# GpSimd's DMA queue in written order: two quarters' sums fetched inside the last period, two behind it

## The chip, the cores and the metric

The kernel runs on one core of one Trainium2 chip. Its time is the device time of one execution in microseconds (us); lower is better. The engines are TensorE (PE; its weight loads are PEld), VectorE (DVE), ScalarE (ACT), GpSimd (POOL) and SyncE (SP), which issues transfers only. Transfers issued by SP go through one queue (q1 in the profile), those issued by GpSimd through another (q0); both are served by the core's 16 DMA engines.

## The reference

One decoder layer is computed for a prompt group (1 x 1024 tokens) and a sample group (8 x 8 tokens) that share weights. What matters here is the layer's last part, the squared-ReLU MLP with a gated residual:

```
h2 = rms_norm(x, norm2_g) * (1.0 + scale2) + shift2
ff = square(relu(h2 @ w_ff1)) @ w_ff2        # 1024 -> 4096 -> 1024
x  = x + gate2 * ff
```

Everything is float32. The outputs are the prompt's and the sample's new x and the states of the layer's earlier parts, which the change does not touch.

## The kernel before, in words

Each float32 matrix product is made of three products of rounded parts (high x high, high x low, low x high). The second MLP product is cut over its inner size of 4096 into NG = 8 groups of 512. For groups 0 to 6 (`for g in range(NG - 1)`, here called the periods) the product for the prompt's 1024 tokens is formed by the seven-product scheme for 2 x 2 blocks: `slot(parts, n, rests)` is product n, with four blocks m of 128 output rows and 512 tokens, six matmuls each. Between the slots lie blocks of the next group's first MLP product (`ff1_items`). The last group, g = 7, is multiplied plainly, after the periods: 16 blocks of 12 matmuls, in the order (i, t) = (0, 0), (0, 1), (1, 0), (1, 1), where i is the half of the output rows and t the half of the tokens.

A product's block lies in one of seven PSUM banks. `add_to(g, n, m, ps)` (line 1431) has ScalarE copy it to a stage in SBUF; after every second block GpSimd issues a transfer that adds the stage to one or two of six sums in DRAM (`kept`, called y_parts in the profile; lines 1442 and, for the first write, 1444). `SUMS` says which:

```python
SUMS = [(0, 1), (2,), (1,), (0,), (4,), (3,), (5,)]
```

So sum 0 is complete after product 3, sums 1 and 2 after product 2, sum 4 after product 4, sum 3 after product 5 and sum 5 after product 6 of the last period. Before, a stage is one whole row block of the tile x1 (rows 5, 6 or 7 in turn, 1024 columns). x1 is a tile of 128 partitions x 8 row blocks x 1088 columns, whose prompt part was saved to DRAM earlier, so that it is free; the 64 columns behind SEQ hold the sample group.

At the end each quarter (i, j) of x1 (row blocks 4i to 4i + 3, token half j) is filled with its sums: (0, 0) from sum 0; (0, 1) from 1, 2, 4; (1, 1) from 1, 2, 3; (1, 0) from 1, 3, 5. Before, SP issues each quarter's first sum (line 1605) as a plain fetch and GpSimd the others as accumulating fetches (line 1603, x<-y_parts in the profile). The saved x comes back in eight loads `xr` (line 1598). Then for each block of the last group DVE computes x = x * gate + xr, then x = ps * gate + x, and SP writes the result (line 1633). `sample_out` and `sample_end` do the same for the sample group; they stand after the blocks m = 3 of (i, 0) and m = 1 of (i, 1).

The order on PE, ACT and DVE is pinned to the program's by `keep_in_program_order` from the periods on (class `InOrder`, `pinned`). Transfers are not pinned before the change: a planner places them on SP's and GpSimd's queues by costs and due times. A transfer waits at its issuing engine until the data that it reads are there and those that it overwrites have been read, and what stands behind it on that engine waits too.

Of the kernel before, what the change touches and what calls it, by code (L numbers as in the profile page):

```python
# [11 lines left out]
ALU = mybir.AluOpType  # L12
# [6 lines left out]
SEQ = 1024  # L19
# [121 lines left out]
def decoder_step(ctx: ExitStack, tc: tile.TileContext, A, O, where):  # L141
    nc = tc.nc
# [21 lines left out]
    ACT, DVE = InOrder(nc.scalar), InOrder(nc.vector)  # L164
# [65 lines left out]
    def mm_psum(w):  # L230
        return bank("mm")[:, :w]
# [27 lines left out]
    def product(ps, hi, lo, act, ks, w0=lambda n: n * P, span=None):  # L259

        n = len(ks)
        for x in range(*(span or (0, n))):
            ah, al = act(ks[x])
            wh, wl = hi[:, w0(x) : w0(x) + P], lo[:, w0(x) : w0(x) + P]
            PE.matmul(ps, wh, ah, start=x == 0, stop=False)
            PE.matmul(ps, wh, al, start=False, stop=False)
            PE.matmul(ps, wl, ah, start=False, stop=x == n - 1)
# [9 lines left out]
    def act_of(tiles, c):  # L277
        return lambda k: (tiles[c][k // 4][0][:, k % 4, :], tiles[c][k // 4][1][:, k % 4, :])
# [50 lines left out]
    with ExitStack() as gctx:  # L329
# [173 lines left out]
        def tick():  # L503
            for entry in list(jobs):
                entry[1] -= 1
                if entry[1] <= 0:
                    wait = next(entry[0], None)
                    if wait is None:
                        jobs.remove(entry)
                    entry[1] = wait  # L510
            for job in start_at.pop(now[0], ()):
                spawn(job())
            pump(0 if now[0] < 10 else 2900 if now[0] < 26 else 1700)
            now[0] += 1
# [599 lines left out]
        def slot(c, i, evac, functions=None):  # L1114
            c0, w = CH[c]
            ps = mm_psum(w)
            product(ps, *ready[i], act_of(h, c), range(8))
            if i >= 4 or c == 2:
                tick()
            if functions:  # L1120
                table(functions)
            evac(IN_BLOCKS[i], c, c0, w, ps)
# [67 lines left out]
        for c, (c0, w) in enumerate(CH):  # L1190
            for j in range(2):
                ps = mm_psum(w)
# [9 lines left out]
            for j in range(2):  # L1202
                o, g = M[:, MA + j, c0 : c0 + w], gate[j][:, c0 : c0 + w]
# [7 lines left out]
    with ExitStack() as fctx:  # L1211
        xp = fctx.enter_context(tc.tile_pool(name="xp", bufs=1))
        x1 = xp.tile([P, 8, NT], F32, tag="x1", name="x1")
# [106 lines left out]
        NG = FF // P // G  # L1320
        H = 512
# [3 lines left out]
        def quarter(g, i, j):  # L1325

            raw = room(RAW[turn["raw"] % 4])
            turn["raw"] += 1
            nc.sync.dma_start(raw.rearrange("p (q f) -> p q f", q=2),
                              A["w_ff2"][g, 2 * i : 2 * i + 2].rearrange("q p f -> p q f")[:, :, H * j : H * j + H])  # L1330
            return raw
# [64 lines left out]
        for c in range(3):  # L1396
            for b in range(G) if c < 2 else (2, 3, 0, 1):
                ps = mm_psum(CH[c][1])
# [27 lines left out]
        kept = nc.dram_tensor("y_parts", (P, 6, 4, H), F32, kind="Internal").ap()  # L1426
        SUMS = [(0, 1), (2,), (1,), (0,), (4,), (3,), (5,)]
        started = set()
        stage = [None]

        def add_to(g, n, m, ps):

            if m % 2 == 0:
                stage[0] = x1[:, 5 + stage[1] % 3, 0:1024]
                stage[1] += 1
            ACT.copy(stage[0][:, (m % 2) * H : (m % 2) * H + H], ps)
            if m % 2:
                src = stage[0].rearrange("p (m t) -> p m t", m=2)
                for a in SUMS[n]:
                    dst = kept[:, a, m - 1 : m + 1]  # L1440
                    if (a, m) in started:
                        nc.gpsimd.dma_start(dst, src, accum_op=ALU.add)  # L1442
                    else:
                        nc.gpsimd.dma_start(dst, src)
                    started.add((a, m))

        stage.append(0)
# [33 lines left out]
        t = first_sum(u)  # L1481

        for g in range(NG - 1):
            nu = Group()
            state = {"f": 0}

            def ff1_items(n):
                for _ in range(n):
                    f = state["f"]
                    state["f"] += 1  # L1490
                    b, c = f // 3, f % 3
                    x = G * (g + 1) + b
                    ps = next_bank()[:, : CH[c][1]]
                    ff1_block(nu, x, c, ps)
                    ff1_out(nu, x, c, ps)
                    if c == 0:
                        ff1_split(x + 1)
                        ff1_load(x + 2)

            def slot(parts, n, rests):  # L1500

                rests = list(rests)
                for m in range(4):
                    ps = next_bank()
                    products(ps, m, *parts, True, True)
                    if rests:
                        rests.pop(0)()
                    add_to(g, n, m, ps)


            DVE.tensor_tensor(out=s, in0=s, in1=a22, op=add)
            w, r0 = form(s, "a")
            v, r1 = form(t, "q")
            parts2 = (w, v)
            slot(now_parts, 0, [r0, r1])
            st = sample_parts(g, u)
            ff1_items(1)
            sm = sample_bank()
            sample_product(sm, st, now_parts[0], 0, True, False)
            ff1_items(1)  # L1520


            DVE.tensor_tensor(out=s, in0=s, in1=a11, op=sub)
            DVE.tensor_tensor(out=t, in0=u.quarter(1, 1), in1=t, op=sub)
            w, r0 = form(s, "a")
            v, r1 = form(t, "q")
            parts3 = (w, v)
            slot(parts2, 1, [r0, r1])
            a11 = quarter(g, 0, 0)
            ff1_items(2)  # L1530


            DVE.tensor_tensor(out=t, in0=u.quarter(1, 0), in1=t, op=sub)
            w, r0 = form(a12, "a")
            v, r1 = form(u.quarter(1, 0), "q")
            parts4 = (w, v)
            slot(parts3, 2, [r0, r1])
            ff1_items(2)


            t3 = u.quarter(0, 1)
            DVE.tensor_tensor(out=t3, in0=u.quarter(1, 1), in1=t3, op=sub)
            DVE.tensor_tensor(out=s, in0=a12, in1=s, op=sub)
            w, r0 = form(s, "a")
            v, r1 = form(u.quarter(1, 1), "q")
            parts5 = (w, v)
            slot(parts4, 3, [r0, r1])
            a21, a22 = quarter(g, 1, 0), quarter(g, 1, 1)
            sample_product(sm, st, parts4[0], 1, False, True)
            sample_out(g, 0, sm)  # L1550
            ff1_items(1)


            DVE.tensor_tensor(out=a11, in0=a11, in1=a21, op=sub)
            w, r0 = form(a11, "a")
            v, r1 = form(t3, "q")
            parts6 = (w, v)
            slot(parts5, 4, [r0, r1])
            nxt = quarter(g + 1, 0, 0)
            ff1_items(2)  # L1560


            w, r0 = form(a22, "a")
            v, r1 = form(t, "q")
            parts7 = (w, v)
            slot(parts6, 5, [r0, r1])
            last = g + 1 == NG - 1
            s = quarter(g + 1, 0 if last else 1, 1 if last else 0)
            ff1_items(1)


            w, r0 = form(a21, "a")
            slot(parts7, 6, [r0])
            sm = sample_bank()
            sample_product(sm, st, parts7[0], 1, True, False)
            sample_product(sm, st, w, 0, False, True)
            sample_out(g, 1, sm)
            if not last:
                a11 = nxt
                now_parts = two(a11, "ah", "al"), two(nu.quarter(0, 0), "qh", "ql")  # L1580
                t = first_sum(nu)
                a22, a12 = quarter(g + 1, 1, 1), quarter(g + 1, 0, 1)
                ff1_items(2)
            else:
                weights, parts = {(0, 0): two(nxt, "ah", "al")}, {(0, 0): two(nu.quarter(0, 0), "qh", "ql")}
                weights[0, 1] = two(s, "wh", "wl")
                ff1_items(1)
                parts[1, 0] = two(nu.quarter(1, 0), "q12", "t")
                ff1_items(1)
            u = nu  # L1590


        g = NG - 1
# [2 lines left out]
        xr = [x.rearrange("p a b -> p (a b)")[:, 0:SEQ] for x in xr]  # L1596
        for m in range(8):
            nc.sync.dma_start(xr[m], save[:, m, :])
        for i, j, terms in ((0, 0, (0,)), (0, 1, (1, 2, 4)), (1, 1, (1, 2, 3)), (1, 0, (1, 3, 5))):
            for n, a in enumerate(terms):  # L1600
                dst = x1[:, 4 * i : 4 * i + 4, H * j : H * j + H]
                if n:
                    nc.gpsimd.dma_start(dst, kept[:, a], accum_op=ALU.add)
                else:
                    nc.sync.dma_start(dst, kept[:, a])

        def sample_end(i):

# [10 lines left out]
        for i in range(2):  # L1619
            for t in range(2):  # L1620
                for m in range(4):
                    ps = next_bank()
# [94 lines left out]
```

## Time and profile before

| | |
|---|---|
| median of 3 runs | 1231.93 us (1228.66 to 1232.12) |
| the profiled execution | 1232.46 us, span 1230.6 us |
| mean granted TensorE clock | 0.993 |
| PE / DVE / ACT / POOL busy | 98% / 52% / 46% / 9% of the span |
| transfers from GpSimd's queue q0 | 65.02 MB |
| transfers from SP's queue q1 | 116.76 MB |

The span runs from the first to the last instruction; the execution's time is 1.9 us longer. Shares are averages over the whole span, and the change concerns the last 120 us and the layout of the stages, so the rows by time matter more than the shares. In rows of a timeline the first number is the start in us from the span's start and the second the length in us; a bracket gives the engine's idle time before the instruction and what ended it. A transfer's row on GpSimd or SP is its issue; its landing is told apart.

### The profile page before, as it was taken

The page shows a single profiled execution, that of the slowest core. Times are in us where ns is not written, and L with a number is a line of the kernel's source. Part 1 is how long each engine was busy: PE and PEld are TensorE (multiplying, and loading weights), DVE is VectorE, ACT ScalarE, POOL GpSimd, SP SyncE. Part 2 cuts the span into 40 slices and gives each one's busy share as a digit, 9 for nine tenths or more (in the row PEclk, how much of TensorE's full clock was granted, in tenths as well). Part 3 has the DMA queues.
Part 4 walks back from the last instruction along what each step waited for, and adds up shares of the span by engine and source line. Part 5 has one row for each costly group of instructions (what it writes and reads, how often), then busy time and mean ns, then how long its engine had stood idle before and what let it go on. Part 6 is the DMA issues. An engine that isn't in the chain of part 4 may idle for free.

```text
span 1230.6 us, 17492 instructions
## 1 busy us (share of the span) xinstructions
PE 1211.3 (98%) x7054; PEld 1099.4 (89%) x7054; DVE 639.4 (52%) x1006; ACT 566.8 (46%) x1137; POOL 107.8 (9%) x146
## 2 busy tenths in 40 slices
PE   8999999999999999999999999999999999999897
PEld 6888789998899999999999899999999999999785
DVE  4789798884786538433243343333324334333254
ACT  4452333433466316545554554544545555554410
POOL 0000000000000000001011111111111111111110
PEclk9999999999999999999999999999999999999998
DMA  9758711120121722134576787786876877879995
GB/s 345 261 170 293 206 35 36 52 55 18 36 71 64 255 83 88 35 129 128 154 184 137 159 177 144 162 173 131 176 165 137 171 155 156 170 148 196 271 283 136
DMA packets 81576, 182.95 MB, mean 149 GB/s; under 512 B 15448, under 2 KB 31576, under 8 KB 81496
## 3 DMA queue, kind: packets, MB, share of 16 engines
q0 software_dynamic: 19296, 65.02, 29.0%
q1 hardware_dynamic: 62055, 116.76, 29.0%
q8 instruction: 55, 0.90, 0.3%
q14 instruction: 26, 0.21, 0.1%
q10 hardware_dynamic: 144, 0.07, 0.0%
HBM read 112.39 MB, written 69.44 MB: 148 GB/s over the span
## 4 chain that ended last, share of the span: by engine, by line
PE 86%; DMA 4%; DVE 4%; issue 3%; SPq 1%; ACT 1%; POOL 1%; DVEq 0%; POOLq 0%; ACTq 0%
PE ps L171 47%; PE mm L171 29%; PE pm L171 6%; PE sm L171 2%; DMA x<-y_parts 2%; DMA y_parts<-x 2%; PE pm L175 1%; PE ada L171 1%; DMA M<-in_xT 1%; SPq L391 1%; DVE x L158 0%; DVE qh L305 0%; DVE lo L312 0%; DVE ql L305 0%; DVE M L614 0%
## 5 line engine op out<-in xcount | busy, mean ns | idle before, releaser
L171 PE MATMUL ps<-hi,wl 128*128 128x384 f32 (+1 forms) x672 | 219.5, 327 | 0.0
L171 PE MATMUL ps<-hi,wh 128*128 128x384 f32 (+1 forms) x672 | 219.3, 326 | 0.0
L171 PE MATMUL ps<-lo,wh 128*128 128x384 f32 (+1 forms) x672 | 219.1, 326 | 0.0
L171 PE MATMUL mm<-hi,wh 128*128 128x384 f32 (+1 forms) x544 | 181.6, 334 | 0.4 <-ACT hi L158 0.4
L171 PE MATMUL mm<-lo,wh 128*128 128x384 f32 (+1 forms) x544 | 177.7, 327 | 0.5 <-DVE lo L158 0.4
L171 PE MATMUL mm<-hi,wl 128*128 128x384 f32 (+1 forms) x544 | 177.3, 327 | 0.5 <-DVE wl L158 0.5
L171 PE MATMUL ps<-qh,ah 128*128 128x512 f32 x408 | 159.6, 391 | 2.7 <-ACT qh L158 2.1
L171 PE MATMUL ps<-ql,ah 128*128 128x512 f32 x408 | 160.2, 393 | 1.0 <-DVE ql L158 1.0
L171 PE MATMUL ps<-qh,al 128*128 128x512 f32 x408 | 160.1, 392 | 0.0
L158 ACT ACTIVATE q<-ps 128x384 f32<-128x384 f32 (+1 forms) x112 | 42.5, 380 | 237.4 <-PE ps L171 237.4
L158 DVE TENSOR_TENSOR wl<-fr,wh 128x1024 fp32r<-128x1024 f32 x27 | 33.1, 1225 | 191.0 <-ACT wh L158 191.0
L171 PEld LDWEIGHTS ps<-hi,wh 128*128 128x128 f32 x672 | 126.2, 188 | 2.2
L171 PEld LDWEIGHTS ps<-lo,wh 128*128 128x128 f32 x672 | 126.2, 188 | 2.2
L1442 POOL DMA_DIRECT2D y_parts<-x x100 | 86.5, 933 | 462.0 <-ACT x L158 460.3
L171 PEld LDWEIGHTS ps<-hi,wl 128*128 128x128 f32 x672 | 126.1, 188 | 0.0
L158 ACT COPY x<-ps 128x512 f32<-128x512 f32 x196 | 106.5, 585 | 38.2 <-PE ps L171 26.1
L171 PEld LDWEIGHTS mm<-hi,wh 128*128 128x128 f32 x544 | 102.1, 188 | 8.9 <-issue 6.4
L171 PEld LDWEIGHTS mm<-lo,wh 128*128 128x128 f32 x544 | 102.2, 188 | 1.4 <-DVE lo L158 1.4
L171 PEld LDWEIGHTS mm<-hi,wl 128*128 128x128 f32 x544 | 102.0, 188 | 1.0 <-DVE wl L158 1.0
L614 DVE SCALAR_TENSOR_TENSOR M<-glu,cmix,M 128x512 f32<-128x512 f32 (+2 forms) x150 | 97.7, 666 | 2.0
L171 PEld LDWEIGHTS ps<-qh,ah 128*128 128x128 f32 x408 | 76.9, 189 | 17.9 <-ACT qh L158 2.4
L171 PEld LDWEIGHTS ps<-ql,ah 128*128 128x128 f32 x408 | 77.0, 189 | 16.2 <-DVE ql L158 1.3
(346 smaller groups left out, 1905.8 us busy)
## 6 DMA issues: line engine op xcount, KB each, us to landing
y_parts<-x POOLq DMA_DIRECT2D x112, 512.0 KB, 7.2
w<-in_w_ff SPq DMA_DIRECT2D x29, 512.0 KB, 3.9
ar<-in_w_ff SPq DMA_DIRECT2D x28, 512.0 KB, 5.2
fr<-in_w_ff SPq DMA_DIRECT2D x28, 512.0 KB, 3.6
w<-in_w_in SPq DMA_DIRECT2D x22, 512.0 KB, 5.2
M<-in_ada SPq DMA_DIRECT2D x20, 512.0 KB, 5.0
ada<-in_ada SPq DMA_DIRECT2D x16, 512.0 KB, 10.5
x<-y_parts POOLq DMA_DIRECT2D x6, 1024.0 KB, 12.4
```

The lines of the kernel that those rows point to most:

```text
L158: i = f(*args, **kw)
L171: return tc.keep_in_program_order(nc.tensor.matmul(*args, **kw))
L175: return tc.keep_in_program_order(nc.tensor.transpose(*args, **kw))
L391: nc.sync.dma_start(t.rearrange("p (a k) -> p a k", a=4), src)
L614: DVE.scalar_tensor_tensor(dst, src(t), cdw[:, j, t : t + 1], dst, ALU.mult, ALU.add))))
L1442: nc.gpsimd.dma_start(dst, src, accum_op=ALU.add)
```

## The change

Three things are changed. The stages move: a stage is now two row blocks x 512 columns, in turn (6, 7) of token half 1, (4, 5) of half 1, and (6, 7) of half 0, all in the quarters (1, 0) and (1, 1). All transfers that GpSimd issues in this part, the writes of partial sums included, are pinned to the order of the program. And all fetches of sums are issued by GpSimd: sum 0 into quarter (0, 0) after product 3 of the last period (g == NG - 2), sums 1 and 2 into (0, 1) after product 4, and after the period sum 4 into (0, 1), then 1, 3, 5 into (1, 0), then 1, 2, 3 into (1, 1).

```diff
+        def queued(dst, src, more):
+
+            tc.keep_in_program_order(nc.gpsimd.dma_start(dst, src, **({"accum_op": ALU.add} if more else {})))
+
+        def gather(i, j, terms, more=False):
+
+            for a in terms:
+                queued(x1[:, 4 * i : 4 * i + 4, H * j : H * j + H], kept[:, a], more)
+                more = True
+
         def add_to(g, n, m, ps):
 
             if m % 2 == 0:
-                stage[0] = x1[:, 5 + stage[1] % 3, 0:1024]
+                stage[0] = (x1[:, 6:8, H:SEQ], x1[:, 4:6, H:SEQ], x1[:, 6:8, 0:H])[stage[1] % 3]
                 stage[1] += 1
-            ACT.copy(stage[0][:, (m % 2) * H : (m % 2) * H + H], ps)
+            ACT.copy(stage[0][:, m % 2], ps)
             if m % 2:
-                src = stage[0].rearrange("p (m t) -> p m t", m=2)
+                src = stage[0]
                 for a in SUMS[n]:
                     dst = kept[:, a, m - 1 : m + 1]
-                    if (a, m) in started:
-                        nc.gpsimd.dma_start(dst, src, accum_op=ALU.add)
-                    else:
-                        nc.gpsimd.dma_start(dst, src)
+                    queued(dst, src, (a, m) in started)
                     started.add((a, m))
...
             slot(parts4, 3, [r0, r1])
+            if g == NG - 2:
+                gather(0, 0, (0,))
...
             slot(parts5, 4, [r0, r1])
+            if g == NG - 2:
+                gather(0, 1, (1, 2))
...
         for m in range(8):
             nc.sync.dma_start(xr[m], save[:, m, :])
-        for i, j, terms in ((0, 0, (0,)), (0, 1, (1, 2, 4)), (1, 1, (1, 2, 3)), (1, 0, (1, 3, 5))):
-            for n, a in enumerate(terms):
-                dst = x1[:, 4 * i : 4 * i + 4, H * j : H * j + H]
-                if n:
-                    nc.gpsimd.dma_start(dst, kept[:, a], accum_op=ALU.add)
-                else:
-                    nc.sync.dma_start(dst, kept[:, a])
+        gather(0, 1, (4,), True)
+        gather(1, 0, (1, 3, 5))
+        gather(1, 1, (1, 2, 3))
```

## The prediction

> **What bounds the kernel now.** I read the first page's engine line, then its chain, then the chain of waits in order of time over the last 230 us, then the timelines of GpSimd, ScalarE, VectorE and TensorE for the end.
>
> ```profile
> span 1230.6 us, 17492 instructions
> ...
> PE 1211.3 (98%) x7054; PEld 1099.4 (89%) x7054; DVE 639.4 (52%) x1006; ACT 566.8 (46%) x1137; POOL 107.8 (9%) x146
> ...
> q0 software_dynamic: 19296, 65.02, 29.0%
> ...
> y_parts<-x POOLq DMA_DIRECT2D x112, 512.0 KB, 7.2
> ```
>
> TensorE (PE) is busy for 98% of the span, so in the seven periods nothing else can matter unless it stops PE. GpSimd's queue (q0) carries 65 MB, most of it 112 writes of partial sums that land 7.2 us after issue (median), and its engine is 9% busy. The end is different. In the chain of waits, a start, a length and an owner per row, PE is the owner up to 1125 us, and then come transfers:
>
> ```profile
> 1121.24 4.20 PE ps L171 x24
> ...
> 1134.11 9.22 DMA y_parts<-x
> ...
> 1163.75 10.23 DMA y_parts<-x
> ...
> 1198.41 11.78 DMA x<-y_parts
> ...
> 1226.87 0.75 DVE x L158
> ```
>
> So the last write of partial sums lands at 1163.75 + 10.23 = 1174.0, fetching starts after it, and the last fetch (x<-y_parts) lands at 1198.41 + 11.78 = 1210.2. VectorE (DVE), the second stall of PE and its consequences are in these rows of the DVE and PE timelines and of a table by windows (PE, PEld, DVE, ACT, POOL busy, PEclk, DMA share, GB/s):
>
> ```profile
> 1194.39 0.75 DVE L158 SCALAR_TENSOR_TENSOR x<-ps,mod,x 128x512 f32<-128x512 f32 x1 [1.31 <-PE ps L171]
> 1210.21 0.75 DVE L158 SCALAR_TENSOR_TENSOR x<-x,mod,xr 128x512 f32<-128x512 f32 x1 [15.07 <-DMA x<-y_parts]
> ...
> 1216.27 0.68 DVE L158 TENSOR_TENSOR acc<-sm,acc 128x512 f32<-128x512 f32 x1
> ...
> 1212.09 0.39 PE L171 MATMUL ps<-fr,al 128*128 128x512 f32 x1
> 1217.01 1.96 PE L171 MATMUL ps<-pair,acc 128*128 128x64 f32 x8 [4.53 <-DVE acc L158]
> ...
> 1226.21 0.39 PE L171 MATMUL ps<-q,ah 128*128 128x512 f32 x1
> 1226.44 0.39 PE L171 MATMUL ps<-fr,al 128*128 128x512 f32 x1
> ...
> 1150.00:1160.00 10.00, 10.00 (x52) 9.06 (x51) 1.92 (x2) 1.35 (x3) 0.85 (x1) 1.00 1.09 284
> ...
> 1220.00:1225.00 5.00, 5.00 (x15) 3.92 (x15) 2.25 (x5) 0.00 (x0) 0.00 (x0) 0.61 0.28 81
> ```
>
> DVE waits 15.07 us for quarter (1,0). Its sample update stands behind the four blocks of that quarter, so PE stops for 4.53 us, and afterwards runs at a granted clock of 0.61. Fetches, not products, own this end.
>
> The GpSimd timeline shows in what way its queue is single file (idle before an instruction and what ended it in brackets); the ScalarE rows show the copies that feed it:
>
> ```profile
> 1121.59 1.30 POOL L1603 DMA_DIRECT2D x<-y_parts  x1 [12.66 <-DMA x<-y_parts]
> 1122.35 2.32 POOL L1442 DMA_DIRECT2D y_parts<-x  x2
> 1133.14 1.82 POOL L1442 DMA_DIRECT2D y_parts<-x  x2 [8.47 <-ACT x L158]
> 1145.13 1.29 POOL L1603 DMA_DIRECT2D x<-y_parts  x1 [10.17 <-issue]
> 1145.90 2.30 POOL L1442 DMA_DIRECT2D y_parts<-x  x2
> ...
> 1180.38 1.30 POOL L1603 DMA_DIRECT2D x<-y_parts  x1 [15.79 <-DVE wl L158]
> 1184.02 1.30 POOL L1603 DMA_DIRECT2D x<-y_parts  x1 [2.34 <-DMA x<-y_parts]
> ...
> 1117.93 1.67 ACT L158 COPY x<-ps 128x512 f32<-128x512 f32 x3
> ...
> 1141.67 1.67 ACT L158 COPY x<-ps 128x512 f32<-128x512 f32 x3
> ...
> 1162.38 1.07 ACT L158 COPY x<-ps 128x512 f32<-128x512 f32 x2 [10.74 <-DMA y_parts<-x]
> ```
>
> An accumulating fetch is issued only when the earlier fetch into the same quarter has landed, and while it waits, the writes behind it wait too (1121.59, then 1122.35). Prices of one fetch of 1 MB, each from a window that holds that one (the line after each is its time to landing): alone on GpSimd, beside an SP fetch and output writes, twice queued behind another accumulation, and a plain SP fetch alone.
>
> ```profile
> L1603 POOL DMA_DIRECT2D x<-y_parts x1: 1304/1304/1304, 1121.6 to 1121.6; - x1
> DMA to landing us min/median/max: 8.5/8.5/8.5
> L1603 POOL DMA_DIRECT2D x<-y_parts x1: 1300/1300/1300, 1180.4 to 1180.4; - x1
> DMA to landing us min/median/max: 11.2/11.2/11.2
> L1603 POOL DMA_DIRECT2D x<-y_parts x1: 1296/1296/1296, 1184.0 to 1184.0; - x1
> DMA to landing us min/median/max: 14.1/14.1/14.1
> L1603 POOL DMA_DIRECT2D x<-y_parts x1: 1285/1285/1285, 1191.9 to 1191.9; - x1
> DMA to landing us min/median/max: 13.0/13.0/13.0
> L1605 SPq DMA_DIRECT2D x<-y_parts x1: 367/367/367, 1116.0 to 1116.0; - x1
> DMA to landing us min/median/max: 5.0/5.0/5.0
> ```
>
> **What the change costs, part by part.**
>
> *Two chains become one.* Beyond the last period the old kernel has two chains in flight, (1,1) and (1,0), with first terms from SP at about 1174, and GpSimd alternating between them. Their landings were 1180.4 + 11.2 = 1191.6, 1184.0 + 14.1 = 1198.1, 1191.9 + 13.0 = 1204.9 and 1210.2: 6.5, 6.8 and 5.3 us apart, mean 6.2. One chain's latency was covered by the other's transfer. In the new order GpSimd issues sum 4 into (0,1); sums 1, 3, 5 into (1,0); only then sums 1, 2, 3 into (1,1). Each accumulation waits for the landing before it, so its whole time to landing counts: between 8.5 (alone) and 11.2 (shared), plus about 0.4 until issue (1184.02 + 14.1 landed at 1198.1, the next issue was 1198.41). In the new order output writes run beside it but no SP fetch, so I take 9.4 + 0.4 = 9.8, nearer to the first row. A fetch that needs no wait adds only its transfer: 5.9 for an accumulation (between 5.3 and 6.8, nearer to the first, which had no SP fetch beside it), 3.5 for a plain one (below the 5.0 alone, above half of the 5.9).
>
> *The fetches that move into the period.* Quarter (0,0) is issued when the writes of product 3 have landed. These now go at about 1119 to 1121, as their copies end (1117.93 and after), for the fetch that held them until 1122.35 is gone; with 7.2 us to landing the fetch starts near 1129 and lands near 1134, before the writes of product 4 (1133.14) are much delayed. Sum 1 into (0,1) follows at about 1135, lands behind those writes at about 1146 (9.22 from 1134.11 gives 1143.3; without SP's fetch some 1 to 2 less; plus 3.5). Sum 2 then goes at about 1146.5. What is queued behind it are the writes of product 5, whose first copies end near 1143: they go at about 1147 instead of 1145.90. ScalarE waits for exactly this write to land (the 10.74 us before 1162.38); behind its copies stand the casts for the last products, so PE waits with it. Cost here +1 us, between -2 (if sum 1 lands early and the writes go at 1143.5) and +4 (if it lands near 1150). The cover is thin: the two copies of a product leave some 8 us of queue time, and this fetch takes them.
>
> *Removed from SP.* Four first fetches of 367 ns of issue. SP's weight fetches that stood behind them gain at most some us, but PE waited for none of them at this place. Nothing.
>
> *Stages.* Three stages remain three; ScalarE waited for a stage only in the 10.74 us above. A row of a write's source is now two pieces of 512 elements, not one of 1024. The accumulating fetches have such pieces: 1 MB in 8.5 alone, of which 5.9 is transfer, so 512 KB would land in 8.5 - 2.95 = 5.5, where the old writes have 7.2. The price per write lies between a gain of 1.7 and a loss of 2.95 (if the pieces came wholly on top), on a queue that is 29% used, with GpSimd pausing 8.47 us before a pair (1133.14): I take zero in the periods. That the written order replaces a planner's order changes nothing there, because the writes already go as their copies end.
>
> *Sum.* The last write lands at 1174.0 + 1 (later issue) + 1 (more in its queue) = 1176. Sum 4 into (0,1): +5.9 = 1181.9. Sum 1 into (1,0): +3.5 = 1185.4. Sums 3 and 5: +19.6 = 1205.0, five us earlier than before. Sum 1 into (1,1): +3.5 = 1208.5. Sums 2 and 3: +19.6 = 1228.1. PE no longer stops: the sample update is done by 1205.0 + 6.06 + 0.68 = 1211.7, before PE asks for it at 1212.5 (1212.09 + 0.39), so PE is done by about 1219 (24 products 0.23 apart, as the rows at 1226.21 and 1226.44, are 5.5, and 1 for the small ones). But the last quarter now ends the program. DVE does its four blocks in 6.06 (1210.21 to 1216.27) and the sample tail in 0.8; then an output of 2.0 and 0.9 to the end:
>
> ```profile
> DMA to landing us min/median/max: 2.0/2.0/2.1
> ```
>
> 1228.1 + 6.06 + 0.8 + 2.0 + 0.9 = 1237.9 of span, +7.3 against 1230.6. The profiled execution's time was 1232.46, 1.9 over its span, and 0.5 above the median 1231.93. Prediction 1231.93 + 7.3 = 1239.2; I say 1240, because the window from 1150 to 1160 shows the DMA engines full (1.09), where one more transfer can only lengthen a queue.
>
> With every accumulation at 8.5 and no later last write, six us go: about 1233. With all four at 11.2 it is 1247.
>
> **A rule beside it.** The Trainium skill, "DMA: Bandwidth & Descriptors", section "Anatomy of one DMA", gives a fit of 2.0 us plus bytes over 436 GB/s, which is 4.4 us (an estimate from that page) for 1 MB. The plain fetch of 5.0 roughly agrees; the accumulating one of 8.5 does not, and by the fit the last quarter would land near 1202 and the kernel would gain as in the first rival. The same page's "Issuing engines are not separate DMA queues" says that where a transfer is issued matters only for the issue time; by that rule the move from SP costs nothing by itself, which holds for bytes but leaves out the wait that GpSimd's order adds.
>
> **The rivals.**
>
> *Faster: the last quarter is in time.* If fetches in one queue overlap so that (1,1) lands by 1212, PE's end decides: the 4.53 us and the slow clock go, PE ends near 1219 instead of 1226.83, DVE, output and end follow: 1219 + 0.75 + 2.0 + 0.9 = 1222.7 of span, 1224 of time. For it: transfers back to back take only 5.9. Against it: GpSimd waited 2.34 us for a landing before it issued the fetch of 1184.02, and 12.66 us before that of 1121.59. It decides where the four accumulations take under 5.8 us each. Chance 0.10.
>
> *No change.* Accumulations at 8.5, the last write where it was: (1,1) lands at 1174.0 + 5.9 + 3.5 + 17.8 + 3.5 + 17.8 = 1222.5, span 1232.3, time 1233.6 (inside 1228.2 to 1235.6). For it: 8.5 is a row of this trace. Against: output writes of quarters (0,0) and (0,1) run beside the first two. Chance 0.17.
>
> *Much slower: the copies wait longer.* If sum 1 into (0,1) lands near 1150, product 5's writes are 4 us later, ScalarE's wait grows from 10.74 to some 15, PE and everything behind shift by 4: with accumulations as I price them, 1243; with 11.2, 1250. Chance 0.18.
>
> *The forecast*, 1236 to 1244: chance 0.55.
>
> **How the numbers follow.** Faster by over 0.3% (about what a measurement of this kernel tells from none, 3.7 us): 0.10. Within: 0.17. Slower: 0.55 + 0.18 = 0.73. The range leaves out the faster rival and the top of the slow one: 1231 to 1247.
>
> **What would show it.** On GpSimd, after the last write, seven x<-y_parts issues in a row, four gaps that end with a landing of x<-y_parts, and the last landing near 1228. DVE's wait moves from quarter (1,0) to (1,1) and is the longest of the end; PE has no 4.53 us gap near 1212 and no clock of 0.61 at 1220. ScalarE's wait for y_parts is 10 to 13 us. The prediction is wrong if the last accumulation lands before 1221, or if ScalarE's wait is gone.

## The result and the profile after

The changed kernel takes 1239.25 us (median of 5 runs, 1238.42 to 1239.82) against 1232.12 for the kernel before (5 runs): ratio 1.006, 95% interval 1.0045 to 1.0076. It is slower by 7 us. The profiled execution took 1239.57, its span is 1237.8, so the difference of spans, 7.2, is the one to be explained.

From the first page of the changed kernel:

```profile
span 1237.8 us, 17479 instructions
...
PE 1207.7 (98%) x7054; PEld 1096.6 (89%) x7054; DVE 639.2 (52%) x1006; ACT 567.3 (46%) x1137; POOL 148.1 (12%) x150
...
q0 software_dynamic: 33184, 69.21, 31.9%
...
y_parts<-x POOLq DMA_DIRECT2D x112, 512.0 KB, 7.7
```

PE's busy time is lower than before, by 3.6 us, and yet the span is longer. GpSimd's queue has four fetches of 1 MB more and many more packets, the two-piece stages; a write lands in 7.7 us and not 7.2 (median). In the periods that costs nothing: the first write behind 1105 us is issued at 1106.87 before and at 1107.06 now. The table by windows for 540 to 1100 us, first of the changed kernel, then of the kernel before:

```profile
540.00:1100.00 560.00, 560.00 (x2959) 513.79 (x2958) 207.17 (x186) 295.12 (x554) 117.30 (x102) 1.00 0.76 161
```

```profile
540.00:1100.00 560.00, 560.00 (x2959) 513.82 (x2958) 207.15 (x186) 294.69 (x554) 83.41 (x102) 1.00 0.73 161
```

PE has the same 2959 matmuls in the same 560 us; only GpSimd's issuing grew, from 83 to 117 us, under cover. What costs time happens after 1100. GpSimd's timeline there:

```profile
1129.68 0.80 POOL L1433 DMA_DIRECT2D x<-y_parts  x1 [7.04 <-DMA y_parts<-x]
1133.33 2.49 POOL L1433 DMA_DIRECT2D y_parts<-x  x2 [2.85 <-ACT x L158]
1135.37 1.25 POOL L1433 DMA_DIRECT2D x<-y_parts  x1
1148.39 1.28 POOL L1433 DMA_DIRECT2D x<-y_parts  x1 [11.77 <-DMA x<-y_parts]
1149.15 4.16 POOL L1433 DMA_DIRECT2D y_parts<-x  x3
1168.73 1.20 POOL L1433 DMA_DIRECT2D y_parts<-x  x1 [15.42 <-ACT x L158]
1169.46 1.79 POOL L1433 DMA_DIRECT2D x<-y_parts  x1
1172.84 0.80 POOL L1433 DMA_DIRECT2D x<-y_parts  x1 [1.59 <-DMA y_parts<-x]
1186.89 1.27 POOL L1433 DMA_DIRECT2D x<-y_parts  x1 [13.25 <-DMA x<-y_parts]
1196.21 2.04 POOL L1433 DMA_DIRECT2D x<-y_parts  x2 [8.04 <-DMA x<-y_parts]
1209.06 1.27 POOL L1433 DMA_DIRECT2D x<-y_parts  x1 [10.80 <-DMA x<-y_parts]
1219.24 1.27 POOL L1433 DMA_DIRECT2D x<-y_parts  x1 [8.91 <-DMA x<-y_parts]
```

After the last write (1168.73) stand the seven fetches, and from 1186.89 on four of them wait for the landing of the fetch before. The first of the seven, sum 4 into (0,1) at 1169.46, is itself new in this place: the planner had issued it inside the last period (the row at 1145.13 of the kernel before, landed at 1158.9), so both quarters of the first half were complete there before the last write landed. Now it lands at 1183.1, in front of the two quarters that matter. What the fetches hold up is in the timelines of ScalarE, TensorE and VectorE:

```profile
1167.36 1.07 ACT L158 COPY x<-ps 128x512 f32<-128x512 f32 x2 [15.53 <-DMA y_parts<-x]
...
1170.38 0.79 PE L171 MATMUL ps<-qh,ah 128*128 128x512 f32 x1 [6.94 <-ACT qh L158]
...
1222.83 0.39 PE L171 MATMUL ps<-fr,al 128*128 128x512 f32 x1
...
1206.20 0.75 DVE L158 SCALAR_TENSOR_TENSOR x<-x,mod,xr 128x512 f32<-128x512 f32 x1 [6.70 <-DMA x<-y_parts]
1227.64 0.75 DVE L158 SCALAR_TENSOR_TENSOR x<-x,mod,xr 128x512 f32<-128x512 f32 x1 [14.70 <-DMA x<-y_parts]
```

Quarter (1,0) arrives at 1206.2, 4 us earlier than before, and PE is through at 1223.2 (1222.83 + 0.39), 3.6 us earlier than before, although it had lost 6.94 us in front of the last products (2.15 before). But quarter (1,1) arrives at 1227.6, and DVE's four blocks, the output and the end take the last 10 us. The kernel no longer ends with PE but with its last fetch; the experiments test whether that is the whole loss.

### The profile page after: what moved, and what is told of

Read it like the earlier page. It is cut to its first block, busy times and chain, and to the rows that moved or that the text cites. A ratio compares the mean times of both kernels' runs of the same rounds, so it can differ in the third digit from the quotient of the medians.

```text
span 1237.8 us, 17479 instructions
## 1 busy us (share of the span) xinstructions
PE 1207.7 (98%) x7054; PEld 1096.6 (89%) x7054; DVE 639.2 (52%) x1006; ACT 567.3 (46%) x1137; POOL 148.1 (12%) x150
## 4 chain that ended last, share of the span: by engine, by line
PE 80%; DMA 6%; issue 6%; DVE 4%; POOL 2%; ACT 1%; SPq 1%; POOLq 0%; DVEq 0%; ACTq 0%
PE ps L171 42%; PE mm L171 29%; PE pm L171 6%; DMA x<-y_parts 4%; PE sm L171 2%; POOL y_parts L1433 1%; PE pm L175 1%; PE ada L171 1%; DMA M<-in_xT 1%; SPq L391 1%; DMA y_parts<-x 1%; DVE x L158 0%; POOL x L1433 0%; DVE qh L305 0%; DVE ql L305 0%
## 5 line engine op out<-in xcount | busy, mean ns | idle before, releaser
L1433 POOL DMA_DIRECT2D y_parts<-x x112 | 129.8, 1281 | 776.8 <-ACT x L158 475.3
L158 DVE TENSOR_TENSOR wl<-fr,wh 128x1024 fp32r<-128x1024 f32 x27 | 33.1, 1225 | 190.9 <-ACT wh L158 190.9
L171 PEld LDWEIGHTS ps<-qh,ah 128*128 128x128 f32 x408 | 76.9, 188 | 22.7 <-ACT qh L158 7.2
L171 PEld LDWEIGHTS ps<-qh,al 128*128 128x128 f32 x408 | 76.9, 188 | 16.1
```

The costliest lines, as they stand in the source:

```text
L158: i = f(*args, **kw)
L171: return tc.keep_in_program_order(nc.tensor.matmul(*args, **kw))
L1433: tc.keep_in_program_order(nc.gpsimd.dma_start(dst, src, **({"accum_op": ALU.add} if more else {})))
```

## The experiments

Three explanations were set against each other: the single file of the last fetches (S), ScalarE's longer wait and the PE gap before the last products (F), and the two-piece stages (L). All runs are compared with the kernel before on the same chip: 1231.78 us in the first four, 1232.31 in the next four, 1231.41 in the last three. Times are medians; spans and rows are those of the one execution that was profiled. In these the end begins at slightly different times (the first write behind 1105 us is issued between 1105.84 and 1107.25), so the place of single rows of two runs can be compared only to about 1.4 us.

| run | median us | ratio to before, 95% |
|---|---|---|
| e1_two_chains | 1229.43 | 0.9989 (0.9977 to 1.0002) |
| e2_drop_last | 1230.12 | 0.9994 (0.9979 to 1.0008) |
| e3_layout_only | 1226.76 | 0.9964 (0.9952 to 0.9976) |
| e4_order_only | 1239.05 | 1.0069 (1.0054 to 1.0085) |
| e5_four_stages | 1240.05 | 1.0068 (1.0053 to 1.0082) |
| e6_early | 1237.82 | 1.0051 (1.0034 to 1.0068) |
| e7_both | 1227.82 | 0.9966 (0.9954 to 0.9979) |
| e8_both_four | 1227.85 | 0.9969 (0.9958 to 0.9980) |
| e9_sp_first | 1231.82 | 1.0008 (0.9995 to 1.0021) |
| e10_sp_two_chains | 1230.29 | 0.9992 (0.9980 to 1.0004) |
| e11_early_sp_two_chains | 1225.81 | 0.9958 (0.9942 to 0.9974) |

**Alternating chains (e1_two_chains).** Same fetches, same queue, same engine; only the order of the last six changes.

```diff
         gather(0, 1, (4,), True)
-        gather(1, 0, (1, 3, 5))
-        gather(1, 1, (1, 2, 3))
+        for n in range(3):
+            gather(1, 0, ((1, 3, 5)[n],), n > 0)
+            gather(1, 1, ((1, 2, 3)[n],), n > 0)
```

> The changed kernel, with its last six fetches issued in turn for quarters (1,0) and (1,1) (sum 1, sum 1, then 3 and 2, then 5 and 3) and no longer all of (1,0) first. Theory S (single file: the serial waits of the last quarter's fetches set the end): quarter (1,1) lands near 1213 and not at 1227.6, so PE's end decides (its last product ended at 1223.2 in the changed kernel, plus 0.75 for DVE and 2.9 for output and end): span near 1227, time near 1228.5, 10 below the changed kernel and 3 below the kernel before. Rival F (front: ScalarE's longer wait of 15.5 us and the PE gap of 6.9 us before the last products set the end): those stay as they are, so span stays at 1237 to 1239. Rival L (layout: writes in two pieces slow GpSimd's queue): unchanged too, 1236 to 1239.

Measured: 1229.43, span 1226.0, 10 us below the changed kernel. Rows of the timelines of GpSimd, TensorE and VectorE in this run:

```profile
1195.13 1.27 POOL L1433 DMA_DIRECT2D x<-y_parts  x1 [5.03 <-DMA x<-y_parts]
1202.07 1.26 POOL L1433 DMA_DIRECT2D x<-y_parts  x1 [5.67 <-DMA x<-y_parts]
...
1167.63 0.80 PE L171 MATMUL ps<-qh,ah 128*128 128x512 f32 x1 [5.28 <-ACT qh L158]
...
1221.63 0.39 PE L171 MATMUL ps<-fr,al 128*128 128x512 f32 x1
...
1208.58 0.75 DVE L158 SCALAR_TENSOR_TENSOR x<-x,mod,xr 128x512 f32<-128x512 f32 x1 [11.15 <-DMA x<-y_parts]
```

Quarter (1,1) lands at 1213.6, where 1213 was put. The PE gap in front is still 5.28 us, but DVE waits for one quarter only, and PE ends the program again. F and L fall as explanations of the 7 us.

**One link less (e2_drop_last).** Sum 3 is left out of quarter (1,1).

```diff
-        gather(1, 1, (1, 2, 3))
+        gather(1, 1, (1, 2))
```

> The changed kernel without its very last fetch (sum 3 is not added into quarter (1,1), so that quarter's values lack a term); nothing else differs. Theory S: the last landing moves from 1227.6 to 1219, and the span falls by the 8.4 + 0.3 of that one link, to about 1229 (PE's end allows 1227). Rival F: the end is PE's, nothing moves: 1237 to 1239. Rival L: 1 MB less in the queue but only behind everything else: 1236 to 1239.

Measured: 1230.12, 9.1 us below the changed kernel; span 1229.6, against a forecast of 1229. One link of the file is worth 8.2 us of span.

**Each half of the change by itself.** The layout alone, on the kernel before (e3_layout_only):

```diff
-                stage[0] = x1[:, 5 + stage[1] % 3, 0:1024]
+                stage[0] = (x1[:, 6:8, H:SEQ], x1[:, 4:6, H:SEQ], x1[:, 6:8, 0:H])[stage[1] % 3]
...
-            ACT.copy(stage[0][:, (m % 2) * H : (m % 2) * H + H], ps)
+            ACT.copy(stage[0][:, m % 2], ps)
...
-                src = stage[0].rearrange("p (m t) -> p m t", m=2)
+                src = stage[0]
```

> The kernel before with one part of the change alone: the new place of the stages (two row blocks x 512 columns in the last two quarters); the planner's order and SP's four first fetches stay. Theory S: two chains still alternate at the end, so the time is that of before within 2 us (1230 to 1234). Rival L: most of the 7 us come from the layout, 1236 to 1239. Rival F says nothing sure here: 1230 to 1236, as ScalarE's wait comes out.

Measured: 1226.76, ratio 0.9964. All three expectations are missed: the layout alone is a gain of 5 us. The timelines of SP, GpSimd and VectorE in this run show what changed:

```profile
1164.62 0.37 SPq L1605 DMA_DIRECT2D x<-y_parts  x1
...
1170.73 0.37 SPq L1605 DMA_DIRECT2D x<-y_parts  x1
...
1173.23 1.30 POOL L1603 DMA_DIRECT2D x<-y_parts  x1 [10.29 <-DMA xr<-x_save]
1187.07 2.58 POOL L1603 DMA_DIRECT2D x<-y_parts  x2 [12.54 <-DMA x<-y_parts]
1203.62 1.27 POOL L1603 DMA_DIRECT2D x<-y_parts  x1 [13.96 <-DMA x<-y_parts]
...
1198.27 0.75 DVE L158 SCALAR_TENSOR_TENSOR x<-x,mod,xr 128x512 f32<-128x512 f32 x1 [6.50 <-DMA x<-y_parts]
```

With the old layout both first fetches of the last two quarters waited for the very last write (1174.1). Now (1,0) holds only the stage whose last write belongs to product 5, and SP fetches its first sum at 1164.62, beside the last writes. The quarter arrives at 1198.27 and not at 1210.21, and PE's 4.53 us gap goes. GpSimd's order changed with it, for the planner places these fetches anew: both accumulations of (1,0) (1173.23 and the first of the two at 1187.07) now stand before those of (1,1). In the kernel before, (1,1) was complete first, at 1204.9, although DVE needs (1,0) first. So the two chains do not alternate here, against the expectation; only (1,1)'s first accumulation goes out together with (1,0)'s last. How much of the 5 us is the earlier first sum and how much the new order, no run tells apart.

The order alone, on the changed kernel with the old stages (e4_order_only):

```diff
-                stage[0] = (x1[:, 6:8, H:SEQ], x1[:, 4:6, H:SEQ], x1[:, 6:8, 0:H])[stage[1] % 3]
+                stage[0] = x1[:, 5 + stage[1] % 3, 0:1024]
...
-            ACT.copy(stage[0][:, m % 2], ps)
+            ACT.copy(stage[0][:, (m % 2) * H : (m % 2) * H + H], ps)
...
-                src = stage[0]
+                src = stage[0].rearrange("p (m t) -> p m t", m=2)
```

> The changed kernel with the old place of the stages (one row block x 1024 columns, rows 5 to 7): the order of the queue alone. Theory S: the same single file, started a little later because sum 1 into (1,0) must now wait for the last write to land: 1238 to 1242. Rival L: back to 1230 to 1233. Rival F: 1236 to 1240, as ScalarE's wait stays long.

Measured: 1239.05. The whole loss is there without the new layout: it belongs to the written order and to the first fetches' move to GpSimd's queue. Under this order the layout's 5 us are worth nothing (1239.25 with it): the fetch that it frees early stands in GpSimd's queue behind the last writes and sum 4, and sum 1 of (1,0) lands at 1186.0 without the layout and at 1186.6 with it. L is out; S and F both allow this time.

**The front by itself (e5_four_stages).** A fourth stage takes ScalarE's wait away and leaves the queue as it is.

```diff
-                stage[0] = (x1[:, 6:8, H:SEQ], x1[:, 4:6, H:SEQ], x1[:, 6:8, 0:H])[stage[1] % 3]
+                stage[0] = (x1[:, 6:8, H:SEQ], x1[:, 4:6, H:SEQ], x1[:, 6:8, 0:H], x1[:, 4:6, 0:H])[stage[1] % 4]
```

> The changed kernel with a fourth stage (row blocks 4 and 5 of token half 0), so that ScalarE's copies of product 6 reuse a stage whose write landed at about 1145 and no longer wait for 1167. Theory S (single file at the end): ScalarE's wait of 15.5 us and the PE gap of 6.9 us go, but the last writes still stand in the same full queue and land at 1175 to 1178, the seven fetches behind them land as before, the last at 1225 to 1228: span 1235 to 1238. Rival F (the front gap sets the end): span falls by the 7 to 8 us of the gap, to 1230 or less.

Measured: 1240.05, no gain. From its timelines:

```profile
1153.80 1.20 POOL L1433 DMA_DIRECT2D y_parts<-x  x1 [1.54 <-ACT x L158]
...
1188.03 1.27 POOL L1433 DMA_DIRECT2D x<-y_parts  x1 [16.26 <-DMA x<-y_parts]
...
1228.12 0.75 DVE L158 SCALAR_TENSOR_TENSOR x<-x,mod,xr 128x512 f32<-128x512 f32 x1 [14.68 <-DMA x<-y_parts]
```

The last write is issued 15 us earlier than in the changed kernel (1153.80, was 1168.73), the PE gap of 6.94 is gone (PE stops for 8.44 us behind the sample update instead), and sum 3 of (1,0) is nevertheless issued at 1188.03, 1.1 us later than there. The last write takes 25.4 us to land, where it took 9.3: issued earlier into this queue, it only waits longer. F is out as the setter of the end.

**The two gathers in the period exchanged (e6_early)**, so that no accumulation stands in front of product 5's writes:

```diff
-                gather(0, 0, (0,))
+                gather(0, 1, (1, 2))
...
-                gather(0, 1, (1, 2))
+                gather(0, 0, (0,))
```

> The changed kernel with its two gathers inside the last period exchanged: sums 1 and 2 into (0,1) after product 3, sum 0 into (0,0) after product 4; the end stays single file. Theory S: the write of product 5 that ScalarE waits for goes at 1143 to 1144 and not at 1149, ScalarE's wait falls under 5 us, the last writes are issued some 13 us earlier and land near 1167, so the same single file ends 10 to 11 us earlier: last landing near 1217, span 1226 to 1229. Rival F gives a gain too, but no more than the PE gap: 1229 to 1231, with the last landing staying above 1222.

Measured: 1237.82, a gain of 1.4 us (span 1234.7, 3.1 less), where some 10 were expected. ScalarE's wait did fall, to 7.42 us and not under 5; the last write was issued 9 us earlier, at 1159.77, but sum 3 of (1,0) still only at 1184.29:

```profile
1159.77 1.19 POOL L1433 DMA_DIRECT2D y_parts<-x  x1 [7.30 <-ACT x L158]
...
1184.29 1.27 POOL L1433 DMA_DIRECT2D x<-y_parts  x1 [20.57 <-DMA x<-y_parts]
...
1224.55 0.75 DVE L158 SCALAR_TENSOR_TENSOR x<-x,mod,xr 128x512 f32<-128x512 f32 x1 [14.34 <-DMA x<-y_parts]
```

My step had reckoned the landing from the issue, and the backlog of the queue decides it. From the issue of that sum 3 to the arrival of (1,1) the file takes 1227.64 - 1186.89 = 40.8 us in the changed kernel, 40.1 with four stages and 40.3 here: nearly the same in all three, whatever happens before.

**Both (e7_both: the exchange and the alternating chains), and both with four stages (e8_both_four).**

> The exchange of e6_early and the two alternating chains of e1_two_chains. Theory S: last landing near 1204, before PE's end; PE without its gap before the last products and without the stall behind the sample update ends near 1214 to 1217, span 1217 to 1221, time 1219 to 1223: 10 below the kernel before. Rival F: the same as e6_early within 2 us, because only the front counted.

> e7_both with the fourth stage of e5_four_stages. If a rest of ScalarE's wait is left in e7_both, it goes: 1 to 3 us below e7_both. If e7_both has no such wait, equal to it within 1 us; 1219 to 1222 either way.

Measured: 1227.82 and 1227.85. The alternating chains bring the 10 us again (1237.82 to 1227.82), but the 1219 to 1223 are missed: (1,0) arrives at 1206.6 in the one and 1206.2 in the other, and PE stops behind the sample update for 5.6 and 7.8 us, first in e7_both, then in e8_both_four:

```profile
1213.41 1.97 PE L171 MATMUL ps<-pair,acc 128*128 128x64 f32 x8 [5.58 <-DVE acc L158]
```

```profile
1212.96 1.97 PE L171 MATMUL ps<-pair,acc 128*128 128x64 f32 x8 [7.83 <-DVE acc L158]
```

What PE gains in front it gives back there. The fourth stage removed a ScalarE wait of 7.05 us that e7_both still had and brought nothing, against its expectation of 1 to 3 us.

**SP issues the two plain first fetches again (e9_sp_first)**, everything else as in the changed kernel:

```diff
+        for i, j in ((1, 0), (1, 1)):
+            nc.sync.dma_start(x1[:, 4 * i : 4 * i + 4, H * j : H * j + H], kept[:, 1])
         gather(0, 1, (4,), True)
-        gather(1, 0, (1, 3, 5))
-        gather(1, 1, (1, 2, 3))
+        gather(1, 0, (3, 5), True)
+        gather(1, 1, (2, 3), True)
```

> The changed kernel with only the plain first fetches of (1,0) and (1,1) issued by SP again; GpSimd keeps its written order for the accumulations, (1,0) wholly before (1,1). Theory S, sharpened by the runs so far: the plain fetches leave the file (3.5 us each) and stand in SP's queue, not behind the last writes and sum 4; sum 3 into (1,0) then lands near 1190, sum 5 near 1199, sum 2 into (1,1) goes without a wait and lands near 1206, sum 3 near 1216: span 1225 to 1228, 10 to 12 below the changed kernel. If the place of issue is worth only issue time (a queue is a queue), the end stays at 1235 to 1238.

Measured: 1231.82, 7.4 us below the changed kernel (span 1228.6, 9.2 less), with (1,0) still wholly before (1,1). The forecast of 10 to 12 was a little too high. Rows of GpSimd:

```profile
1177.86 1.28 POOL L1433 DMA_DIRECT2D x<-y_parts  x1 [10.27 <-DMA x<-y_parts]
1192.05 2.55 POOL L1433 DMA_DIRECT2D x<-y_parts  x2 [12.91 <-DMA x<-y_parts]
1209.24 1.27 POOL L1433 DMA_DIRECT2D x<-y_parts  x1 [14.64 <-DMA x<-y_parts]
```

Sum 3 of (1,0) goes at 1177.86, 9 us earlier, and at 1192.05 two fetches are issued at once, since (1,1) has its first sum by then. The Trainium skill, "DMA: Bandwidth & Descriptors", section "Issuing engines are not separate DMA queues", lets one expect only the time of issue from such a move. Here it is worth 7 to 9 us, for two reasons that the traces show.

The first is that a transfer in SP's queue does not stand behind GpSimd's backlog. SP issues sum 1 into (1,0) at 1166.21, 0.4 us after GpSimd's sum 4, and it lands at 1177.3, 5.7 us before that one; it takes 11.1 us, where GpSimd's took 13.8.

The second is what the waiting fetch holds up behind it on SP. The planner has put four loads of the saved x (`xr`) behind that fetch, so they go at 1166.68; in the changed kernel they go at 1157.70. From 1160 to 1170 the queues (packets, MB, share of the 16 DMA engines' time) move, first in the changed kernel, then here:

```profile
q0 software_dynamic: 596, 1.15, 62.3%
q1 hardware_dynamic: 475, 1.70, 45.7%
```

```profile
q0 software_dynamic: 980, 1.91, 108.6%
q1 hardware_dynamic: 61, 0.09, 3.0%
```

With SP's loads out of the way, the write of product 5 that sum 1 into (1,0) waits for lands 18.3 us after its issue and not 22.7. It is the same elsewhere: 21.6 and 22.2 us in e1_two_chains and e2_drop_last, where the loads go early, 17.5 in e10_sp_two_chains, where they stand behind the fetch. So of the 9.3 us by which that sum lands earlier, 2.7 are the fetch itself, 4.4 the faster write, 1.9 an earlier issue of that write (which lies before the edit) and 0.3 the issue of the fetch; without the 1.9 it is 7.4, as by the medians. No run holds back the loads alone, so this division is read from rows and not tested.

**SP's first fetches and alternating chains**, without (e10_sp_two_chains) and with (e11_early_sp_two_chains) the exchange in the period:

> e9_sp_first with the accumulations of (1,0) and (1,1) alternating. Theory S: PE's end decides, as in e1_two_chains, but without its rest of waiting: span 1224 to 1227. If alternating was the whole gain of e1_two_chains and SP adds nothing: equal to it, 1226 to 1228.

> e7_both with the first fetches of (1,0) and (1,1) issued by SP. e7_both still had PE wait 5.6 us behind the sample update for quarter (1,0), which landed at 1206.6. With its first fetch in SP's queue from about 1164 that quarter lands near 1197, PE's stall goes, PE ends near 1217: span 1220 to 1222, time 1222 to 1224, the fastest of all. If instead the DMA engines' bytes are the limit whatever the queue, span 1225 to 1227 as e7_both.

Measured: 1230.29 (span 1228.2) and 1225.81 (span 1222.9). The first is no better than the alternation alone (1229.43), and misses its forecast of 1224 to 1227: (1,0) arrived at 1209.3, and PE waited 2.72 us for the sample update. Its GpSimd row shows why the two remedies do not add up:

```profile
1193.31 2.55 POOL L1433 DMA_DIRECT2D x<-y_parts  x2 [15.62 <-DMA x<-y_parts]
```

The two are sum 2 into (1,1) and sum 5 into (1,0). Sum 2 waits for (1,1)'s first sum, which SP could issue only behind the last write (1174.89) and which lands at 1192.8; sum 5 into (1,0), which DVE needs first, stands behind it. The second is the fastest of all, ratio 0.9958, ahead of both kernels and level with e3_layout_only inside the intervals. Its forecast was too low, by 1 to 3 us of span, and its mechanism only half right: (1,0) arrived at 1205.6 and not 1197, again with its sum 5 behind sum 2 of (1,1), and PE still waited behind sample updates, 4.1 us together, but there was no gap in front. The exchange with SP's first fetches and (1,0) wholly first was not run.

## Why the prediction was right

The forecast was 1240 (sum 1239.2), measured 1239.25. Point by point, predicted and measured:

| step | predicted us | measured us |
|---|---|---|
| fetch of sum 2 into (0,1) issued | 1146.5 | 1148.39 |
| product 5's first write issued | 1147 | 1149.15 |
| ScalarE's wait | 10 to 13 | 15.53 |
| last write lands | 1176 | 1168.73 + 9.3 = 1178.0 |
| sum 3 into (1,0) issued | 1185.4 + 0.4 | 1186.89 |
| (1,0) complete | 1205.0 | 1206.2 |
| PE's end | 1219 | 1223.2 |
| (1,1) complete | 1228.1 | 1227.6 |
| span | 1237.9 | 1237.8 |

The landing of the last write is from the window that holds it alone:

```profile
L1433 POOL DMA_DIRECT2D y_parts<-x x1: 1196/1196/1196, 1168.7 to 1168.7; - x1
DMA to landing us min/median/max: 9.3/9.3/9.3
```

*Right, and tested:* the two chains that became one. An accumulation and its issue took 9.3, 10.0 (1196.21 to 1206.2), 10.2 (1209.06 to 1219.24) and 8.4 us, mean 9.5, where 9.8 was put. (The row of 8.5 that the prediction calls alone had two writes issued right behind it, at 1122.35.) That the DVE wait would move to (1,1), that PE's 4.53 us would go and that PE would end well before the program: all seen. The granted clock from 1220 to 1225 us, 0.61 before, is 1.00.

*Right sign, wrong size:* the front. The fetch of sum 1 landed at 1147.5 where about 1146 was put, and the issue after it took 0.9 where 0.5 was put, so product 5's writes went 3.25 us later than before and not 1. That is the mechanism of the rival "much slower", whose ScalarE wait of 15 us came true; PE lost 6.94 us in front, and so ended at 1223.2 and not at 1219. The last write landed 4.1 us later than before where the sum had put 2.

The rival's time of 1243 did not come, because the file behind the last write was 2.5 us shorter than put: sum 4 added 5.1 us and not 5.9, the plain sum 1 into (1,1) 2.6 and not 3.5, and the last two accumulations 18.9 and not 19.6. And ScalarE's wait does not set the end: e5_four_stages has none and ends no earlier. So 2 us too little in front and 2.5 too much behind cancelled, with 0.4 more than put after the last landing. The mechanism was right, but the agreement to 0.1 us of span is luck.

*Wrong:* the stages. I priced the layout by its packets alone and took zero. By itself it is worth 5 us, by what it sets free and by the order that the planner then chooses. The sum came out because the written order cannot use it.

The rival "faster" needed accumulations under 5.8 us; they took 8.4 to 10.2. "No change" needed 8.5 for each and a last write that lands where it did; one of the four came to that, and the write landed 4.1 us later.

## What to carry to other kernels

Where transfers depend on each other by pairs, issue the steps of two chains in turn: here six fetches in another order, with not a byte less, were worth 10 us. Count what an in-order queue holds behind a waiting issue, on either queue: a plain fetch moved to the other queue passed the backlog there, but it also held up that queue's own loads, which here happened to help. The remedies are not to be added up without looking at which fetch then waits in front of which. When buffers move, ask first which later transfer they set free, and whether the order lets that transfer go.

## What was not expected of the hardware

An earlier issue into a full queue bought nothing: the last write went 15 us earlier in e5_four_stages, landed 1.1 us later, and sum 3 of (1,0) behind it was issued 1.1 us later. And a transfer from SP passed older ones of GpSimd: in e9_sp_first a fetch issued 0.4 us after one of GpSimd's landed 5.7 us before it. In e3_layout_only the fetch that SP issued at 1164.62 among GpSimd's writes let its quarter's next fetch go at 1173.23, while in the changed kernel the same fetch, issued by GpSimd at 1172.84 behind the last writes and sum 4, did so only at 1186.89.
